# A second feed-forward block's down product turned round, and a final norm taken by token

## Chip, cores and metric

One core of one Trainium2 chip runs the whole program. The metric is device time in microseconds (us), median of the runs shown.

## What is computed

One layer on 512 tokens of width 1024, all in float32: a feed-forward block, a token mixer, a second feed-forward block, and a norm.

```python
x = x + 0.5 * swiglu(rmsnorm(x, ffn1_norm), ffn1_w_gate, ffn1_w_up, ffn1_w_down)
x = x + token_mixer(rmsnorm(x, mix_norm), w_in, w_out, ...)
x = x + 0.5 * swiglu(rmsnorm(x, ffn2_norm), ffn2_w_gate, ffn2_w_up, ffn2_w_down)
return rmsnorm(x, final_norm)
# swiglu(x, g, u, d) = (silu(x @ g) * (x @ u)) @ d, hidden width 2816 = 22 tiles of 128
```

## The kernel before

Between the stages x lies turned: eight tiles `x[k]` of 128 features by 512 tokens. Every product is made of three matmuls (`mm3`, L125): each operand is split into a high part (a cast to fp32r on ScalarE, ACT) and a rest (value minus high part, a subtraction on VectorE, DVE), and high times high, high times rest and rest times high are added in a PSUM bank. TensorE (PE) runs the matmuls, SyncE (SP) and GpSimd (POOL) issue the loads.

A feed-forward block (`ffn`, L207) first computes gate and up products of hidden tiles 0 to 3 with 512 tokens moving (L688 to L717), then hands over to `pipeline` (L636). That one works through a list of **units** (L304 to L322):

- a g or u unit, named by its first hidden tile (g4, g6, u6, g8, ...): the gate or up product of two hidden tiles, done as a two-by-two block product with **seven** products in place of eight. Its steps are in `SEVEN` (L46), named by the weight side: a11, s3, s2, a12, s1, a22, s4. A step is 12 matmuls, 256 tokens moving, and goes to one of four banks w, x, y, z. After a11 the bank w is copied into x, after s2 x into y (L464, L466, ACT), so that later steps add to them: seed copies.
- a d unit: the down product of two output tiles over a group of eight hidden tiles, by the same seven steps. There are two groups (hidden tiles 6 to 13 and 14 to 21) and four d units in each.
- a p unit: an output tile's down product over the first six hidden tiles, in the plain way: 18 matmuls, 512 tokens moving. In the second block, output tiles 6 and 7 do this at the very end by halves of the tokens (l and r, L472), so that the norm of the first half runs beside the second.

The second block's order is g4; g6,u6 to g12,u12; three p; four d; g14,u14 to g20,u20; three p; four d; l and r.

The order on every engine is written out by hand, from a calendar: `starts` gives each step a nominal time (a step is 1410 ns), and events are put at times before it and sorted (`at`, L413). For step t the weight cast on ACT (`high`, L380) is queued four steps ahead, the rest on DVE (`low`, L396) three steps ahead, the sum of weights that s2 and s4 need (`total`, L370) five steps ahead, and a unit's loads seven ahead (L656). Two weight sums of a unit (for s1 and s3) come from memory: SP loads one block, and POOL issues a load that adds the other (L342). Raw weights have three buffers; the split ones have room for six steps. Engines take their queues strictly in this order, each as fast as its inputs come.

`kept` (L542) turns a pair's two activations into what a d unit needs: sums of their four blocks, high parts and rests, 4 operations on ACT and 8 on DVE. Pair (4,5) only gets plain high parts and rests (L558), and so do the single tiles 0 to 3 (`activated`, L223).

After the last group each finished x tile is squared, weighted by the norm's gain and, by halves of the tokens, scaled by the factor; the right half is transposed on TensorE in the end (L1396 to L1549). The output is put together from the two halves.

Of the kernel before, what the change touches and what calls it, by code (L numbers as in the profile page):

```python
# [21 lines left out]
P = 128  # L22
# [31 lines left out]
STEP, PLAIN_STEP, HALF_STEP = 1410, 4080, 2130  # L54
# [12 lines left out]
def tile_macaron(ctx: ExitStack, tc, xs, xT, wf, wgu1, wst1, wd1, wdg1, wqk, wvw, wv, wo, wgu2, wst2, wd2,  # L67
                 wdg2, lams, relb, addc, out):
# [138 lines left out]
    def ffn(wgu, wst, wd, wdg, n0, n1, norm, early, res, nm, hooks, ended, first=None,  # L207
            bias=None, last=None, bank_of_last=None):
# [20 lines left out]
        def gate(j, pg, pu):  # L229
            t1 = tp.tile([P, S], F32, tag="ptb", name=f"t1{nm}{j}")  # L230
# [10 lines left out]
            activated(j, t1)  # L241
# [56 lines left out]
        ups, up_w = {}, {}  # L298
# [5 lines left out]
        units = [("g", n1)]  # L304
        for j in range(n1 + 2, PLAIN + 8, 2):
            units += [("g", j), ("u", j)]
        plain = 5 if last is None else 3
        units += [("p", m) for m in range(plain)] + [("d", 0, m) for m in range(0, KD, 2)]
        for j in range(PLAIN + 8, JF, 2):
            units += [("g", j), ("u", j)]  # L310
        units += [("p", m) for m in range(plain, KD if last is None else KD - 2)]
        units += [("d", 1, m) for m in range(0, KD, 2)]
        if last is not None:
            units += [(h, m) for h in "lr" for m in (KD - 2, KD - 1)]
        ops, begin, starts, now = [], {}, [], 0
        for u in units:
            begin[u] = len(ops)
            for o in ((u[0],),) if u[0] in "plr" else SEVEN:
                ops.append((u, o))
                starts.append(now)  # L320
                now += {"p": PLAIN_STEP, "l": HALF_STEP, "r": HALF_STEP}.get(u[0], STEP)
        starts.append(now)  # L322
# [7 lines left out]
        def sum_slots(u):  # L330
            if u[0] == "d":
                return GROUP_SUMS[u[2] // 2 % 2]
            if u == units[0]:
                return PAIR_SLOTS[0][:2]
# [5 lines left out]
        sums, raws, second, made, half, g, hs = {}, {}, {}, {}, [], {}, {}  # L340
# [12 lines left out]
        def load(u):  # L353
            raws[u] = []
            whole = [wd[u[1]]] if u[0] in "pl" else [rows(u)[0], rows(u)[1][:, 512:]]
            for a in whole:
# [4 lines left out]
        def source(t):  # L361
            u, o = ops[t]
            r0 = raws[u][0]
            if o[0] in ("p", "l"):
                return r0[:, :PLAIN * P]
# [4 lines left out]
        def total(t):  # L370

            u, o = ops[t]
# [6 lines left out]

        def high(t):  # L380
            u, o = ops[t]
            if o[0] in ("p", "l"):
                half.clear()
                h, l = w_place(ODD * (o[0] == "l"))
                made[t] = h[:, :PLAIN * P], l[:, :PLAIN * P]
            else:
                if not half:
                    h, l = w_place(ODD)
                    half.extend([(h[:, :512], l[:, :512]), (h[:, 512:], l[:, 512:])])
                    if t and ops[t - 1][1][0] == "p":  # L390
# [5 lines left out]
        def low(t):  # L396
            h, l = made[t]
            V.tensor_tensor(l, source(t), h.bitcast(F32), op=ALU.subtract)  # L398

# [37 lines left out]
        def product(t):  # L437
            u, o = ops[t]
            if o[0] in ("l", "r"):
                half_product(t, u[1], o[0])  # L440
# [31 lines left out]
        def half_product(t, m, o):  # L472
            c = left if o == "l" else right
            h, l = made[t] if o == "l" else made[t - 2]
            begun = m == KD - 1
            po = bank_of_last(int(o == "r")) if begun else mm_bank(f"p{o}{nm}{m}")
            for k in range(PLAIN):
                w = slice(k * P, (k + 1) * P)
                mm3(po[:, :HS], h[:, w], l[:, w], ah[k][:, c], al[k][:, c],
                    k == 0 and not begun, k == PLAIN - 1, begun)  # L480
                last(starts[t], m, o, k, put)
            if not begun:
                put(starts[t + 1], stt, x[m][:, c], po[:, :HS], 0.5, x[m][:, c], ALU.add)
            last(starts[t + 1], m, o, PLAIN, put)

        def bank_tags(u):


            seq = [v for v in units if v[0] not in "plr"]
# [52 lines left out]
        def kept(j, t1, t0, t2):  # L542
# [11 lines left out]
            def parts(t, h, l, a):  # L554
# [3 lines left out]
            if j < PLAIN:  # L558
                for r, t in ((1, t1), (0, t2)):
                    h = ah[j + r] = slot(j + r, f"ah{nm}{j + r}", F32R)  # L560
                    l = al[j + r] = slot(JF + j + r, f"al{nm}{j + r}", F32R)
                    parts(t + STEP, h[:], l[:], g[j][r][:])
                return
            places = [lambda n=n, i=i: slot(i, f"h{n}{nm}{j}", F32R)
                      for n, i in enumerate(PAIR_SLOTS[(j - PLAIN) // 2 % 4])]
            t = {}

            def b11():
                t["b"] = places[0]()
                A.copy(t["b"][:, left], g0[:, left])  # L570

# [4 lines left out]
            def b2_rest():  # L576
                t["l2"] = places[2]()
                rest(t["l2"][:], g1[:], t["h2"][:])

# [4 lines left out]
            def t0_rest():  # L584
                t["l0"] = places[4]()
                rest(t["l0"][:], g0[:], t["h0"][:])

# [4 lines left out]
            def t1_rest():  # L592
                t["l1"] = places[6]()
                rest(t["l1"][:], g1[:], t["h1"][:])
                b = hs[j] = {"b11": (t["b"][:, left], t["b"][:, right])}
                for n, i, c in (("b21", 2, left), ("b22", 2, right), ("t1", 0, left),
                                ("t3", 0, right), ("t4", 1, left), ("t2", 1, right)):
                    b[n] = t[f"h{i}"][:, c], t[f"l{i}"][:, c]

            put(t0 + STEP, b11)  # L600
            put(t0 + 2 * STEP, lambda: rest(t["b"][:, right], g0[:, left], t["b"][:, left]))
            put(t1 + STEP, b2)
            n = max(t1, t2)
            put(n, less, g0[:, left], g0[:, left], g0[:, right])
            put(n + STEP, b2_rest)
            put(n + STEP, less, g0[:, right], g1[:, right], g0[:, right])
            put(n + 2 * STEP, t0_parts)
            put(n + 2 * STEP, stt, g1[:, right], g1[:, right], -1.0, g0[:, left], ALU.subtract)
            put(n + 2 * STEP, stt, g1[:, left], g1[:, right], -1.0, g1[:, left], ALU.subtract)

            at(n + 3 * STEP, 5, t1_parts)
            late = 2 * STEP * (j > n1)
            at(n + 3 * STEP + late, 1, t0_rest)
            at(n + 4 * STEP + late, 1, t1_rest)

        def down_step(t, u, o, banks):
# [16 lines left out]
            if group == 1 and o in ("a22", "s4") and (last is None or m < KD - 2):  # L633
                ended(m + (o == "a22"), t, put)

        def pipeline():  # L636
            seen = {}
            for t, (u, o) in enumerate(ops):
                if o[0] in ("p", "l"):
# [3 lines left out]
                elif o[0] != "r":  # L643
                    if t == begin[u]:
                        if u != units[0]:
# [5 lines left out]
                            if u == ("g", PLAIN + 10):  # L651
# [4 lines left out]
                        at(starts[t] - 7 * STEP, 1.5, load, u)  # L656
# [4 lines left out]
                at(starts[t], 4, product, t)  # L661
            if bias is not None:
# [8 lines left out]
            run(1 << 40)  # L671

# [717 lines left out]
    half_gain = sp.tile([P, 1], F32, tag="keep", name="half_gain", bufs=1)  # L1390
    fin = {}

    def half(hh):
        return slice(hh * HS, (hh + 1) * HS)

    def weighted(m, hh):  # L1396

        g2 = m // 2
        if (hh, g2) not in fin:
            fin[hh, g2] = cp.tile([P, S], F32, tag=f"xh{hh * 4 + g2}", name=f"y{hh}{g2}")  # L1400
        if m == KD - 1:
            A.activation(fin[hh, g2][:, half(m % 2)], fin["x7", hh][:, :HS], AF.Copy,
                         scale=half_gain[:])
            return
        A.activation(fin[hh, g2][:, half(m % 2)], x[m][:, half(hh)], AF.Copy,
                     scale=sm[:, 3 * KD + m:3 * KD + m + 1])

    def tile_ended(m, t, put):

        squared(m, t, put, EPS * D / P if m == 4 else None)  # L1410
        for hh in range(2):
            put(t + 2 * STEP, weighted, m, hh)

    def last(t, m, o, k, put):


        hh = int(o == "r")
        c = half(hh)
        if k == PLAIN:
            q = fin.setdefault("sq", {})  # L1420
            if m not in q:
                q[m] = slot(8 + m - (KD - 2), f"sql{m}")
            if m == KD - 1:
                put(t, lambda: A.activation(q[m][:, c], fin["x7", hh][:, :HS], AF.Square, scale=0.5))
            else:
                put(t, A.activation, q[m][:, c], x[m][:, c], AF.Square)
            put(t, weighted, m, hh)
            if o == "l":
                put(t, lambda: V.tensor_tensor(sq[:, c], sq[:, c], q[m][:, c], op=ALU.add))
            if (o, m) == ("r", KD - 1):  # L1430
                put(t, final_end)
        elif (o, m, k) == ("l", KD - 2, 0):
            A.activation(root[:], eps[:], AF.Sqrt)
            V.tensor_scalar_mul(half_gain[:], gain(3, KD - 1), 0.5)
# [226 lines left out]
```

## Time and profile before

| | us |
|---|---|
| runs: median (lowest to highest) | 925.98 (925.86 to 926.51) |
| profiled execution: span from first to last instruction | 924.1 |
| median less span: what lies around it | 1.9 |
| pipeline of the second block begins | 633.06 |
| its down product begins (first p tile) | 722.51 |
| last weight product ends | 915.71 |

A span is from the first to the last instruction of the program; the time of a run also holds what lies around it. The page names instructions by engine, line and tiles (out<-in). Duration is from start to end of one instruction; where an engine overlaps instructions, the distance between starts is shorter. DMA rows give the microseconds from issue to landing.

### The profile page before, as it was taken

To read this page: it belongs to the slowest core of one execution; us is meant where nothing else is said; L and a number is where in the kernel's file an instruction comes from. 1 tells how busy PE (TensorE), PEld (TensorE's weight loads), DVE (VectorE), ACT (ScalarE), POOL (GpSimd) and SP (SyncE) were. 2 spreads that over 40 slices of the span, in tenths; PEclk is the share of its full clock that TensorE was granted. 3 is DMA by queue.
4 is the path that set the end of the run, shared out by engine and by line. 5 is a ranking of instruction groups with operands and counts; after the bars stand their busy time and mean duration, and the time that the engine had idled before them with its cause. 6 is when DMAs were issued, how large, how long until landed. Compare 5 with 4: busy or idle time off the path is not lost.

```text
span 924.1 us, 16880 instructions
## 1 busy us (share of the span) xinstructions
PE 917.2 (99%) x6286; PEld 847.1 (92%) x6286; DVE 726.3 (79%) x1499; ACT 544.3 (59%) x1134; POOL 98.0 (11%) x116
## 2 busy tenths in 40 slices
PE   9999999999999999999999999999999999999997
PEld 7888999999999998888989778889999999999997
DVE  7797887686888897858866556797888777888784
ACT  7455665355665775656757664455666455666573
POOL 0001101112201100000000003110120012210100
PEclk9999999999999999999999999999999999999999
DMA  7455646578757563524343213464774677875542
GB/s 263 124 146 151 160 124 177 137 184 211 196 133 200 152 173 99 153 75 128 99 137 93 69 63 120 115 180 101 183 191 117 161 203 189 201 196 145 144 129 92
DMA packets 59827, 136.61 MB, mean 148 GB/s; under 512 B 6816, under 2 KB 8096, under 8 KB 59744
## 3 DMA queue, kind: packets, MB, share of 16 engines
q1 hardware_dynamic: 45776, 110.14, 36.7%
q0 software_dynamic: 13968, 25.39, 17.5%
q8 instruction: 49, 0.80, 0.4%
q14 instruction: 34, 0.28, 0.1%
HBM read 130.21 MB, written 2.14 MB: 143 GB/s over the span
## 4 chain that ended last, share of the span: by engine, by line
PE 97%; DVE 1%; DMA 0%; issue 0%; DVEq 0%; ACT 0%; SPq 0%
PE pq L126 2%; PE pwo L126 2%; PE pq L128 2%; PE pq L127 2%; PE pk L126 2%; PE pk L128 2%; PE pwo L127 2%; PE pwo L128 2%; PE pk L127 2%; PE pua L128 2%; PE pua L127 2%; PE pua L126 2%; PE pda L127 1%; PE pda L126 1%; PE pub L126 1%; PE pub L127 1%
## 5 line engine op out<-in xcount | busy, mean ns | idle before, releaser
L1108 ACT ACTIVATE pr<-pr,mx 128x128 f32<-128x128 f32 (+3 forms) x64 | 36.0, 563 | 37.1 <-DVE mx L1105 36.9
L1105 DVE CUSTOM_DVE_ANT_0 pr<-sc,strip 128x128 f32<-128x128 f32 (+3 forms) x64 | 30.6, 487 | 18.9 <-PE sc L1103 18.6
L394 ACT CAST w<-s2b 128x512 fp32r<-128x512 f32 x50 | 31.0, 621 | 16.0 <-DVE s2b L376 14.4
L398 DVE TENSOR_TENSOR w<-s2b,w 128x512 fp32r<-128x512 f32 x50 | 34.2, 684 | 7.3 <-ACT w L394 7.3
L394 ACT CAST w<-s2a 128x512 fp32r<-128x512 f32 x46 | 28.6, 621 | 16.1 <-DVE s2a L376 13.2
L398 DVE TENSOR_TENSOR w<-s2a,w 128x512 fp32r<-128x512 f32 x46 | 31.5, 684 | 6.6 <-ACT w L394 6.6
L153 POOL TENSOR_TENSOR sq<-sq,sqt 128x512 f32<-128x512 f32 x7 | 11.0, 1564 | 237.9 <-ACT sqt L152 237.8
L126 PE MATMUL pq<-xh,w 128*128 128x512 f32 x64 | 26.7, 417 | 0.0
L126 PE MATMUL pwo<-mh,w 128*128 128x512 f32 x64 | 25.6, 400 | 0.0
L912 DVE TENSOR_TENSOR w<-raw_qk,w 128x512 fp32r<-128x512 f32 x28 | 19.0, 687 | 8.2 <-ACT w L908 8.1
L128 PE MATMUL pq<-xh,w 128*128 128x512 f32 x64 | 25.1, 392 | 0.0
L126 PE MATMUL pk<-xh,w 128*128 128x512 f32 x64 | 25.1, 392 | 0.0
L127 PE MATMUL pq<-xl,w 128*128 128x512 f32 x64 | 25.1, 392 | 0.0
L128 PE MATMUL pk<-xh,w 128*128 128x512 f32 x64 | 25.0, 391 | 0.0
L127 PE MATMUL pwo<-ml,w 128*128 128x512 f32 x64 | 25.0, 390 | 0.0
L128 PE MATMUL pwo<-mh,w 128*128 128x512 f32 x64 | 25.0, 390 | 0.0
L127 PE MATMUL pk<-xl,w 128*128 128x512 f32 x64 | 24.9, 390 | 0.0
L1102 PE MATMUL sc<-k,q 128*128 128x128 f32 (+3 forms) x64 | 20.7, 324 | 0.0
L1103 PE MATMUL sc<-l,q 128*128 128x128 f32 (+3 forms) x64 | 20.5, 322 | 0.0
L127 PE MATMUL pwgb<-xl,w 128*128 128x256 f32 x72 | 20.2, 281 | 0.0
L128 PE MATMUL pwgb<-xh,w 128*128 128x256 f32 x72 | 20.2, 281 | 0.0
L127 PE MATMUL pxgb<-ttb,w 128*128 128x256 f32 x72 | 20.2, 281 | 0.0
(728 smaller groups left out, 4010.0 us busy)
## 6 DMA issues: line engine op xcount, KB each, us to landing
raw_qk<-wqk_dram SPq DMA_DIRECT2D x16, 512.0 KB, 3.2
raw0bg<-wst_dram SPq DMA_DIRECT2D x9, 512.0 KB, 4.7
raw_gua<-wgu_dram SPq DMA_DIRECT2D x8, 512.0 KB, 3.3
raw0ag<-wst_dram SPq DMA_DIRECT2D x8, 512.0 KB, 4.8
raw0ad<-wdg_dram SPq DMA_DIRECT2D x8, 512.0 KB, 4.2
strip<-bias_rows SPq DMA_DIRECT2D x16, 256.0 KB, 3.7
raw_wo<-wo_dram SPq DMA_DIRECT2D x8, 512.0 KB, 3.3
raw_gub<-wgu_dram SPq DMA_DIRECT2D x8, 512.0 KB, 3.5
```

The lines of the kernel that those rows point to most:

```text
L126: T.matmul(po, wh, mh, start=first, stop=False, skip_group_check=on)
L127: T.matmul(po, wh, ml, start=False, stop=False, skip_group_check=on)
L128: T.matmul(po, wl, mh, start=False, stop=last, skip_group_check=on)
L153: G.tensor_tensor(sq[:], sq[:], t[:], op=ALU.add)
L394: A.copy(made[t][0], source(t))
L398: V.tensor_tensor(l, source(t), h.bitcast(F32), op=ALU.subtract)
L912: V.tensor_tensor(l[:, c:c + 512], raw[:, c:c + 512], h[:, c:c + 512].bitcast(F32), op=ALU.subtract)
L1102: T.matmul(ps[:, :w], qs[:, qi], ks[:, :w], start=True, stop=False)
L1103: T.matmul(ps[:, :w], qs[:, qi], ls[:, :w], start=False, stop=True)
L1105: V.tensor_tensor_reduce(out=pi, in0=ps[:, :w], in1=st["b"][m][:, w - 1::-1], op0=ALU.add, op1=ALU.min, scale=1.0, scalar=3.0e38, accum_ou ...
L1108: A.activation(pi, pi, AF.Exp, scale=-1.0, bias=st["mx"][:, m, i:i + 1], accum_out=st["ls"][:, m, i:i + 1])
```

## The change

The second block's down product is turned: for tokens by output features, an activation block (128 hidden by 128 tokens) is the stationary side and the weights move, 512 output features wide. All 22 hidden tiles now go by seven products, as 11 pairs: a two-by-two block product of (two token halves by two hidden tiles) with (two hidden tiles by two feature halves). There are two turned blocks: t0 over pairs 0, 2, 4, 6, 8, and t1 over pairs 10 to 20, a pair being named by its first tile. The order is g4; g6,u6; g8,u8; t0; g10,u10 to g20,u20; t1. In a block, each of the seven products runs over all its pairs before the next one starts; a step of one pair is `mm3` for two token tiles, 6 matmuls of 512. The p, l and r units are gone, and so are the d units of this block (the first block keeps its own).

x is transposed by TensorE in u8: 32 transposes of 128x128, in two lots, copied back by ACT into the same eight tiles, which then hold tokens by features: tile 4*dh+tt is token tile tt, feature half dh. The banks of a turned block are added to them by DVE.

All pairs' activations go through `kept`; those of tiles 0 to 3 stay in slots from the gate on and are split in g4 to g8, 0.75 steps apart. Loads of raw weights of a pair unit are put seven and five steps ahead, in place of both at seven.

The final norm has tokens on partitions: a square with a sum along the row on ACT, a factor of one column on DVE and ACT, and one operation on DVE that scales by the factor and by a broadcast copy of the gain. In t1's last product (s4) tile 2's matmuls run before tile 3's, so that tile 2 is finished beside them; tiles 0 and 1 are finished after a22. The output is written as it is.

```diff
+        else:
+            units = [("g", n1)] + pairs(n1 + 2, TURNED_PAIRS[0][-1] + 2) + [("t", 0)]
+            units += pairs(TURNED_PAIRS[1][0], JF) + [("t", 1)]
...
             for o in ((u[0],),) if u[0] == "p" else SEVEN:
+                for p in range(len(TURNED_PAIRS[u[1]])) if u[0] == "t" else (0,):
+                    ops.append((u, o, p))
+                    starts.append(starts[-1] + (PLAIN_STEP if u[0] == "p" else STEP))
...
+        def block_product(t):
+            u, o, p = ops[t]
+            ps = TURNED_PAIRS[u[1]]
...
+            pw, pz, pv = b[:2], b[2:4], b[4:]
+            banks = {"a11": pw, "s2": pw, "a22": pw, "s3": pz, "s1": pz, "s4": pz, "a12": pv}[o[0]]
...
+            block_mms(banks, o, ps[p], p, n, h, l, (0, 1))
+            if p == n - 1:
+                block_step(starts[t + 1], u, o[0], pw, pz, pv)
+
+        def block_mms(banks, o, j, p, n, h, l, tiles):
+            fresh = o[0] in ("a11", "s3", "a12")
+            bh, bl = hs[j][o[2]]
+            for tt in tiles:
+                c = slice(tt * P, (tt + 1) * P)
+                mm3(banks[tt], bh[:, c], bl[:, c], h, l, fresh and p == 0, p == n - 1, not fresh)
+
+        def block_step(t, u, o, pw, pz, pv):
+            def into(tt, dh, bank, f):
+                y = x[4 * dh + tt]
+                put(t, stt, y, bank, f, y, ALU.add)
+            for i in range(2):
+                if o == "a11":
+                    into(i, 0, pw[i], 0.5)
+                elif o == "s3":
+                    into(i, 1, pz[i], -0.5)
+                    into(2 + i, 1, pz[i], -0.5)
+                elif o == "s2":
+                    put(t, A.copy, pz[i], pw[i])
...
+        def turn(dh):
+            turned = [mm_bank(f"xt{dh}{tt}") for tt in range(NQ)]
+            for tt in range(NQ):
+                for k in range(4):
+                    T.transpose(turned[tt][:, k * P:(k + 1) * P], x[4 * dh + k][:, tt * P:(tt + 1) * P],
+                                ident[:])
...
+            if final is not None:
+                for dh in range(2):
+                    time = starts[begin["t", 0] - 6 + 3 * dh]
+                    at(time, 5, turn_x, time, dh)
+                for n, j in enumerate((0, 2)):
+                    kept(j, 0, (2 + 9 * n) * STEP, 0, 0.75)
...
+        def block_events(t):
+            u, o, p = ops[t]
+            now = starts[t]
...
+            at(now - 4 * STEP, 3, high, t)
+            at(now - 3 * STEP, 2.5, low, t)
...
+    def factor(tt):
+        v, r, w, h, y = (number(n, tt) for n in (3, 4, 5, 6, 7))
+        V.scalar_tensor_tensor(v, number(1, tt), 1.0 / D, number(2, tt), op0=ALU.mult, op1=ALU.add)
+        A.activation(r, v, AF.Sqrt)
+        V.scalar_tensor_tensor(w, r, r, v, op0=ALU.mult, op1=ALU.add)
+        V.reciprocal(w, w)
+        V.tensor_tensor(h, r, w, op=ALU.mult)
+        V.tensor_tensor(y, h, h, op=ALU.add)
...
+        elif what == "a22":
+            for tt in (0, 1):
+                put(t, square, 1, tt, x[4 + tt])
+            for tt in (0, 1):
+                put(t, factor, tt)
+            for tt in (0, 1):
+                put(t, left_out, tt)
+        elif what.startswith("s4") and what.endswith("1"):
+            i = int(what[3])
+            square(1, 2 + i, banks[i], 0.5)
+            factor(2 + i)
+            right_out(2 + i, banks[i])
```

In the new code the cast is L435, the rest L439, the weight sum L398 (turned) and L403, L405, the add into x L530, the seed copies L518, the transposes L629.

More of the change, by code (lines that the diff above doesn't have):

```diff
@@ L296, in up_weights, with pairs @@
             up_w[j] = get_w(wst[j - n1][1], f"su{nm}{j}")
-        ups, up_w = {}, {}
+        ups, up_w, g = {}, {}, {}
         left, right = slice(0, HS), slice(HS, S)
[L304 to L315, printed above, removed]
+        def pairs(j0, j1):
+            return [(h, j) for j in range(j0, j1, 2) for h in "gu"]
+        plain = 5
+        if final is None:
+            units = [("g", n1)] + pairs(n1 + 2, PLAIN + 8)
+            units += [("p", m) for m in range(plain)] + [("d", 0, m) for m in range(0, KD, 2)]
+            units += pairs(PLAIN + 8, JF)
+            units += [("p", m) for m in range(plain, KD)] + [("d", 1, m) for m in range(0, KD, 2)]
+        else:
+            units = [("g", n1)] + pairs(n1 + 2, TURNED_PAIRS[0][-1] + 2) + [("t", 0)]
+            units += pairs(TURNED_PAIRS[1][0], JF) + [("t", 1)]
+        ops, begin, starts = [], {}, [0]
         for u in units:
             begin[u] = len(ops)
[L318 to L322, printed above, removed]
+            for o in ((u[0],),) if u[0] == "p" else SEVEN:
+                for p in range(len(TURNED_PAIRS[u[1]])) if u[0] == "t" else (0,):
+                    ops.append((u, o, p))
+                    starts.append(starts[-1] + (PLAIN_STEP if u[0] == "p" else STEP))
         def rows(u):
@@ L338, in sum_slots @@
             return PAIR_SLOTS[(u[1] - PLAIN) // 2 % 4][o:o + 2]
-        sums, raws, second, made, half, g, hs = {}, {}, {}, {}, [], {}, {}
+        sums, raws, second, made, half, hs = {}, {}, {}, {}, [], {}
         def weight_sums(u):
@@ L351, in weight_sums, with load @@
                 sums[u].append(t)
[L353 to L356, printed above, removed]
+        def load(u, which=(0, 1)):
+            raws.setdefault(u, [])
+            whole = [wd[u[1]]] if u[0] == "p" else [rows(u)[0], rows(u)[1][:, 512:]]
+            for a in [whole[i] for i in which if i < len(whole)]:
                 t = wp.tile([P, 1024], F32, tag="raw", name=f"raw{len(raws[u])}{nm}{u[0]}")
@@ L400, in moving, with kept_weights @@
+        keeps = {}
+        def kept_weights(p):
+            if p < 4:
+                w = tp.tile([P, 5 * HS], F32R, tag=f"pr{p % 2}", name=f"kw{nm}{p}")
+            else:
+                if "tx" not in keeps:
+                    keeps["tx"] = tp.tile([P, 12 * HS], F32R, tag="tx", name=f"kx{nm}", bufs=1)
+                w = keeps["tx"][:, (p - 4) * 1024:(p - 3) * 1024]
+            return w[:, :512], w[:, 512:1024]
         def moving(u, block):
@@ new lines, in turn, with turn_x @@
+        def turn(dh):
[4 more added lines that the diff above has]
+                                ident[:])
+            return turned
+        def turn_x(t, dh):
+            turned = turn(dh)
+            for tt in range(NQ):
+                put(t + STEP * (tt // 2), A.copy, x[4 * dh + tt], turned[tt][:])
@@ L486, in bank_tags @@
         def bank_tags(u):
-            seq = [v for v in units if v[0] not in "plr"]
+            seq = [v for v in units if v[0] != "p"]
             n = seq.index(u)
@@ L594, in t1_rest, with b11_rest @@
                 rest(t["l1"][:], g1[:], t["h1"][:])
[L595 to L598, printed above, removed]
+                block(("t4", "1"), left)
+                block(("t2", "1"), right)
+                hs[j] = b
+            def b11_rest():
+                rest(t["b"][:, right], g0[:, left], t["b"][:, left])
@@ L671, in pipeline @@
             run(1 << 40)
+        def block_events(t):
+            u, o, p = ops[t]
+            now = starts[t]
+            if o[0] in ("s3", "s1"):
+                at(starts[begin[u]] - TURNED_AHEAD[o[0]][u[1]][p] * STEP, 1, block_load, u, o[0], p)
+            elif o[0] == "a11":
+                at(now - 7 * STEP, 2.2, block_load, u, o[0], p)
+            elif o[0] in ("a12", "a22"):
+                at(now - 8 * STEP, 1.5, block_load, u, o[0], p)
+            if (u[1], o[0]) == (1, "s4"):
+                now = starts[begin[u]] + (20 + 3 * p) * STEP
+            if o[0] in ("s2", "s4"):
+                at(now - 5 * STEP, 2, total, t)
+            at(now - 4 * STEP, 3, high, t)
+            at(now - 3 * STEP, 2.5, low, t)
+            if t == begin[u] and u[1] == 1:
+                at(now + 2 * STEP, 1, final, "begin", now + 2 * STEP, put, None)
         j0 = 0
@@ L1448, in bank_begun @@
-    def bank_begun(hh):
-        fin["x7", hh] = mm_bank(f"px7{hh}")
-        A.activation(fin["x7", hh][:, :HS], x[KD - 1][:, half(hh)], AF.Copy, scale=2.0)
-    def final_sums(hh, src, first, end):
-        n = NQ // 2
-        if first:
-            fin["ps", hh] = pp.tile([P, S], F32, tag="mm", name=f"st_n4{hh}", bufs=4)
-        for i in range(n):
-            c = slice((hh * n + i) * P, (hh * n + i + 1) * P)
-            T.matmul(fin["ps", hh][:, i:i + 1], src[:, c], ones_d[:, 0:1], start=first and i == 0, stop=end,
-                     skip_group_check=True)
```

398 lines of the change are left out of this document (219 added, 179 removed).

## Prediction

> **What bounds the kernel now.** I read the page first, for the engine that never rests and for the chain of work that ended last.
>
> ```profile
> span 924.1 us, 16880 instructions
> PE 917.2 (99%) x6286; PEld 847.1 (92%) x6286; DVE 726.3 (79%) x1499; ACT 544.3 (59%) x1134; POOL 98.0 (11%) x116
> ...
> PEclk9999999999999999999999999999999999999999
> ...
> PE 97%; DVE 1%; DMA 0%; issue 0%; DVEq 0%; ACT 0%; SPq 0%
> ```
>
> TensorE (PE) is busy for 99% of the span at full granted clock, and the chain runs through it. A saved TensorE microsecond is a saved microsecond, if VectorE (DVE) keeps up. Next comes busy time by stretch: stretch, its length, then busy time (count) of PE, PEld, DVE, ACT, POOL, then clock, DMA share and GB/s.
>
> ```profile
> 601.09:620.13 19.04, 19.04 (x86) 15.77 (x84) 18.98 (x31) 9.65 (x15) 2.03 (x3) 1.00 0.59 171
> 643.00:662.87 19.87, 19.87 (x170) 19.87 (x169) 15.40 (x28) 13.06 (x29) 3.43 (x4) 1.00 0.73 179
> 662.87:682.75 19.88, 19.88 (x170) 19.88 (x169) 17.54 (x34) 12.76 (x28) 3.48 (x4) 1.00 0.64 169
> 722.51:734.81 12.30, 12.30 (x57) 10.14 (x55) 9.57 (x17) 4.99 (x9) 1.74 (x2) 1.00 0.56 147
> 734.81:774.57 39.76, 39.76 (x338) 39.76 (x336) 31.62 (x60) 20.44 (x41) 6.94 (x8) 1.00 0.69 175
> 854.09:866.38 12.29, 12.29 (x56) 10.14 (x55) 9.56 (x17) 4.98 (x9) 1.75 (x2) 1.00 0.56 145
> 866.38:906.14 39.76, 39.76 (x337) 39.76 (x336) 33.52 (x63) 27.93 (x57) 3.48 (x4) 1.00 0.45 120
> 906.14:915.55 9.41, 9.41 (x82) 9.41 (x81) 3.98 (x14) 3.81 (x12) 0.00 (x0) 1.00 0.01 2
> ```
>
> By the kernel's order these are: gate and up products 512 wide; g6,u6; g8,u8; three p tiles; four d units; three p tiles; four d units; the l and r halves. TensorE has no gap in any. But VectorE has only 4.5 us of idle time in the second row and 2.3 us in the third: in the pairs it is nearly the bound itself. Its queue in g8, and the product that uses its work (start, duration):
>
> ```profile
> 666.60 0.68 DVE L398 TENSOR_TENSOR w<-s1bg,w 128x512 fp32r<-128x512 f32 x1
> 667.20 0.42 DVE L435 SCALAR_TENSOR_TENSOR g1b<-g1b,g0b 128x256 f32<-128x256 f32 x1
> 667.65 0.42 DVE L435 SCALAR_TENSOR_TENSOR g1b<-g1b 128x256 f32<-128x256 f32 x1
> 667.99 0.68 DVE L398 TENSOR_TENSOR w<-raw1bg,w 128x512 fp32r<-128x512 f32 x1
> 668.60 0.68 DVE L398 TENSOR_TENSOR w<-s2b,w 128x512 fp32r<-128x512 f32 x1
> 669.20 0.68 DVE L376 TENSOR_TENSOR s2b<-s1bu,raw0bu 128x512 f32<-128x512 f32 x1
> ...
> 668.55 0.28 PE L126 MATMUL pygb<-txb,w 128*128 128x256 f32 x1
> ```
>
> Two things are to be seen. First, a 512-wide operation takes 0.68 us but the next starts 0.60 us after it; a 256-wide one costs 0.34, or 0.45 where the next reads its result. Second, the rest (L398) of g8's s1 weights ends at 667.28 and its product starts at 668.55: the lead is 1.27 us, and in these rows TensorE never waits for it.
>
> **Part by part.** (1) Down product. Out go 6 p tiles, 8 d units and the halves: 12.30+39.76+12.29+39.76+9.41 = 113.5 us. In come 11 pairs x 7 products x 2 token tiles x 3 = 462 matmuls 512 wide. Their price is that of 601.09:620.13: 28 groups of three, each on another bank, in 19.04 us, 0.2267 each; so 104.7 us. (The p tiles, 54 in 12.30, give 0.2278.) The gain is **8.8 us**: fewer columns (236,544 for 245,760), and 256 columns cost 0.118 (1.42 us for 12), more than half of 0.227. Token tiles as stationary change nothing in the count: each matmul loads its stationary side in before too (PEld count).
>
> (2) The 32 transposes of x stand in u8, in TensorE's order, with nothing beside them.
>
> ```profile
> 916.81 1.94 PE L1509 MATMUL ft<-ident,y 128*128 128x128 f32 x16
> ...
> L1509 PE MATMUL ft<-ident,y 128*128 128x128 f32 x16 | 1.9, 275 | 0.0
> ```
>
> Sixteen took 1.94 us with the last one's own end: 0.11 each, **+3.5 us**. The eight copies back are ScalarE's; ACT is busy for 64% of g8,u8.
>
> (3) VectorE in g6 to g8. The added work is that pairs (0,1) and (2,3) are now also split into the four-block sums of the seven products (a pair: 3 operations 512 wide, 5 of 256), and pair (4,5) goes the same way instead of two plain rests. I count VectorE's queue from the rest of g6's first weights up to that of g8's s1: 28 wide and 13 half-wide operations in before, 35 and 27 now. At 0.603 and 0.337, with six dependent steps of 0.11, that is 30.9 us, against 18 steps x 1.42 = 25.6. It starts with the 3 steps (4.26) that it is queued ahead, less 0.68 for the last one itself: 3.6. So the rest is 5.3-3.6 = 1.7 us late, and TensorE waits for it. Lower bound: 1.3, if some of the idle time ahead of g6 is used. Upper bound: 3.0, if the stretch must also keep the 1.27 us of lead that before still has at its end. I take **+1.9**, near the sum, since a late engine finds the banks that it reads already full. The wait ends in u8, which has little of such work and the transposes.
>
> (4) VectorE in the turned blocks. After the last a11 product x is added from two banks, after s3 from four (L530 of the new code, the same operation as this row, 512 wide):
>
> ```profile
> L435 DVE SCALAR_TENSOR_TENSOR x<-pdb,x 128x512 f32<-128x512 f32 x6 | 4.1, 692 | 5.7 <-PE pdb L128 5.7
> L394 ACT CAST w<-s2b 128x512 fp32r<-128x512 f32 x50 | 31.0, 621 | 16.0 <-DVE s2b L376 14.4 <-PE pdb L127 1.5
> L835 ACT ACTIVATE sqd<-x 128x512 f32<-128x512 f32 x5 | 3.1, 624 | 2.0 <-DVE x L435 2.0
> L502 ACT ACTIVATE g1b<-rbc_n 128x512 f32<-128x512 f32 x9 | 5.7, 632 | 5.1 <-DVE rbc_n L426 4.6
> L423 ACT COPY pxgb<-pwgb 128x256 f32<-128x256 f32 x9 | 3.2, 357 | 7.1 <-PE pwgb L128 7.1
> ```
>
> Queued behind these adds are the rests of the coming weights. In the first block, from the end of a11 to the rest for the fourth s2 product stand 19 wide operations, a half-wide and a dependent one: 12.3 us and 0.3 for hops, against 8 products x 1.361 = 10.9. So TensorE waits **1.7** there (1.2 to 2.2). In the second block 20 wide ones and 0.8 make 13.2 against 9 x 1.361 = 12.3: **+1.0** (0.6 to 1.4). Elsewhere the sum of a block leaves VectorE free: 35 steps of 1.361 hold 62 wide operations and 8 half-wide, 40 of 47.6 us.
>
> (5) Loads. Seven loads of 256 KB a pair replace the down weights of before, at 192 GB/s in a block (9.2 MB in 47.7 us), where pairs ran at 179.
>
> ```profile
> raw0bg<-wst_dram SPq DMA_DIRECT2D x9, 512.0 KB, 4.7
> s3bg<-wst_dram POOLq DMA_DIRECT2D x9, 256.0 KB, 5.8
> ```
>
> I followed SP's queue past each buffer's last reader: the tightest is the first weights of g10, in whose place the first block's raw weights lie until four steps (5.6 us) before the cast needs them; 4.7 fits. SP and POOL otherwise run well ahead. I cost it at nothing; if a load lands 2 us later, the lead of g10 takes it, and the upper bound is those 2 us. Gates 0 to 3, freed from their casts ahead of g4, gain nothing: TensorE is dense there.
>
> (6) The end.
>
> ```profile
> 915.43 0.28 PE L128 MATMUL px<-ahb,w 128*128 128x256 f32 x1
> ...
> 916.99 0.17 ACT L1469 ACTIVATE lt<-st_n 128x2 f32<-128x2 f32 x1 [0.48 <-PE st_n L1462]
> 917.19 0.34 DVE L1473 SCALAR_TENSOR_TENSOR lw<-lt,st_n 128x1 f32<-128x1 f32 x2
> 917.57 0.17 DVE L1475 RECIPROCAL lw<-lw 128x2 f32<-128x2 f32 x1
> 917.77 0.16 DVE L1476 SCALAR_TENSOR_TENSOR ly<-lt,lw 128x2 f32<-128x2 f32 x1
> 918.02 1.46 ACT L1518 ACTIVATE o<-ft,ly 128x512 f32<-128x512 f32 x2 [0.86 <-DVE ly L1476]
> 918.55 2.32 SPq L1523 DMA_DIRECT2D out_dram<-o  x5
> ```
>
> From the last weight product's end (915.71) to the end of the span are 8.4 us. The new end: tile 2's factor waits on VectorE behind the outputs of tiles 0 and 1 (four 512-wide operations, then five small ones of 0.2), and ScalarE's copy for tile 2 behind that factor, so its square of tile 3 starts about 0.7 late (counted from the end of a22, 8.2 us earlier); square 0.65; factor 1.2; first half out 0.5; three issues 0.48 apart (five begin in 2.32-0.4 us), and what follows the last one's begin as in before (924.1-920.4 = 3.7). That is 0.7+0.65+1.2+0.5+1.0+3.7 = 7.75, **-0.65** (from -1.5 to +0.5).
>
> Sum: -8.8+3.5+1.9+1.7+1.0-0.65 = **-1.35 us**, so a span of 922.75. The span is 924.1 where the median of the runs is 925.98, with 1.9 us around it: **924.6 us**.
>
> **Rivals.** (a) VectorE's lateness does not reach TensorE. For it: before reaches leads of over 3 us, and the first half of each turned block is light. Against: the third row, where VectorE is full. The three waits of 4.6 then shrink to 0 to 1.5: 920.0 to 921.5.
>
> (b) The end on the other side: ScalarE's seed copies, in u6, g8 and u8. Product s2 needs px copied from pw, and in ScalarE's order that copy stands behind a Silu or cast that waits for VectorE: after VectorE's result come 0.63, a half-wide operation, a cast 0.62 and the copy 0.36, pipelined some 1.7 us, while the rest of the weights takes 0.6. Where VectorE is already as late as its lead, each such unit adds 1.1, and g6 too; four make +4.4: 929.0. For it: ACT waited 5.1 us for rbc_n in before. Against: a wait at s2 gives VectorE the same time back, and it needs it two steps later anyway. It decides from a VectorE lead below 1.1 us.
>
> (c) A page's rule. VectorE's next operation starts only when the one before is through: 0.68 and 0.42 each. Counted so, the queue up to g8's s1 is 35.3+0.7 us against 25.6, and its wait 6.8 instead of 1.7; in the blocks 19 x 0.08 and 20 x 0.08 come on top, some 3 in all: 933. The Trainium skill, "VectorE: DVE Perf Modes", The DRAIN you can't avoid, says this; the six rows above speak against it, except for the dependent one.
>
> (d) The change does not do what it says: 512 wide costs twice the 256-wide price (0.2367). Then 109.4 replace 113.5: 929.3. The p tiles speak against it.
>
> (e) A transpose costs its duration, 0.275, not the distance to the next: 8.8 us for 3.5, 929.9. The Trainium skill, "TensorE: Matmul & The Clock Gate", Part 4: PE-mode transpose, gives about 275 ns for one in a kernel. The row of durations agrees, and that of sixteen in 1.94 us says that they overlap.
>
> **How the numbers follow.** A measurement of this kernel can tell about 0.2% (1.85 us) from no change. The sum as it stands, between 924.13 and 927.8 with its bounds: 0.42. Faster by more: 0.35, of it rival (a) 0.22, and 0.13 for my sum with the bounds on the low side (waits of 3.1, the end at -1.5: 922.3). Slower by more: 0.23, of it (b) 0.16, (c) 0.03, (d) 0.02, (e) 0.02. The sum's own range, bounds all on one side, is 922.3 to 927.8. To hold 8 in 10 it reaches from 920.3 (rival a at its best lies below) to 929.2 (half of b, and c to e, above).
>
> **What would show it.** TensorE's idle time between 640 and 672 near 1.9 us, ended by DVE L439; another 1.7 and 1.0 in the fourth s2 product of the blocks; blocks of 0.227 per matmul; transposes 0.11 apart; 7.7 us behind the last product. No idle time there would show (a); idle time of s2 products ended by ACT L518, (b). Wrong altogether would be idle time ended by a DMA.

## The result and the profile after

| | median | runs, lowest to highest | profiled execution |
|---|---|---|---|
| before | 926.34 us | 7, 925.75 to 926.57 | span 924.1 |
| changed | 929.57 us | 7, 928.34 to 931.55 | span 927.8 |

The changed kernel is slower by 0.4%: ratio 1.0036, 95% interval 1.0025 to 1.0047. Forecast were 924.6 us, a little faster, with a range from 920.3 to 929.2. The page of the changed kernel, with the parts that were shown of before:

```profile
span 927.8 us, 16132 instructions
PE 914.2 (99%) x5892; PEld 826.7 (89%) x5892; DVE 736.8 (79%) x1518; ACT 545.4 (59%) x1130; POOL 104.5 (11%) x124
...
PE 88%; DVE 8%; DMA 2%; issue 1%; SPq 1%; ACT 1%; POOL 0%; DVEq 0%; POOLq 0%; ACTq 0%
```

TensorE has 3.0 us less to do, and the span is 3.7 us longer. The chain, 97% TensorE before, now runs for 12% through other units: through VectorE, and for 2% through transfers. Where that is, the table by stretch shows (stretch, length, busy time of PE, PEld, DVE, ACT, POOL, then the granted clock): g6; u6; g8; u8; the first turned block; the pairs g10 to u20; the second turned block; and four microseconds out of that block.

```profile
644.04:656.78 12.74, 10.58 (x87) 10.13 (x86) 12.52 (x26) 9.59 (x21) 1.75 (x2) 1.00 0.45 130
656.78:667.06 10.28, 10.20 (x87) 9.99 (x86) 10.21 (x20) 7.26 (x15) 1.82 (x3) 1.00 1.00 236
667.06:676.99 9.93, 9.93 (x86) 9.93 (x85) 9.86 (x21) 6.53 (x14) 3.43 (x4) 1.00 0.98 220
676.99:690.72 13.73, 13.69 (x119) 13.49 (x118) 7.23 (x14) 9.74 (x22) 3.47 (x4) 1.00 0.93 244
690.72:739.32 48.60, 47.91 (x213) 39.34 (x212) 40.88 (x69) 24.03 (x42) 4.33 (x5) 1.00 0.52 129
739.32:858.59 119.27, 119.27 (x1009) 119.27 (x1008) 101.50 (x189) 74.19 (x156) 24.47 (x28) 1.00 0.83 203
858.59:921.28 62.69, 60.22 (x254) 47.96 (x252) 51.83 (x102) 33.31 (x66) 4.59 (x6) 0.97 0.40 118
884.00:888.00 4.00, 4.00 (x12) 3.12 (x11) 4.00 (x8) 1.67 (x4) 0.00 (x0) 0.57 0.00 0
```

The first block is 1.0 us above its 35 x 1.361 = 47.6, the pairs are as before, and the second block is 5.5 above its 42 x 1.361 = 57.2 (0.2 of it is the end of the last matmul). In g6 VectorE is busy for 12.52 of 12.74 us and TensorE for 10.58. The last row is new: for four microseconds the granted clock is 0.57.

I call a wait the distance between the starts of two matmuls, less the 0.227 or 0.118 that it is without one. In g6 there are two waits of 1.3, with the 0.1 by which the next matmul starts late:

```profile
651.10 0.39 PE L139 MATMUL pygb<-txb,w 128*128 128x256 f32 x1 [1.12 <-ACT pygb L518]
655.25 0.39 PE L139 MATMUL pygb<-xh,w 128*128 128x256 f32 x1 [1.04 <-DVE rbc_n L521]
```

With 0.1 in s2 this makes 2.8 us, and at the end of u6 0.35 come on top. The releasers are to be noted: not a rest (L439), but a seed copy on ScalarE, and the addition on VectorE that reads the bank of s1 before s4 may add to it.

In the second block, VectorE's queue (start, duration), and TensorE from the first two matmuls of the fourth s2 product on, of which the second reads the rest:

```profile
872.51 0.69 DVE L398 TENSOR_TENSOR rab<-sCb,rab 128x512 f32<-128x512 f32 x1
...
878.53 0.68 DVE L439 TENSOR_TENSOR w<-rab,w 128x512 fp32r<-128x512 f32 x1
879.14 2.47 DVE L530 SCALAR_TENSOR_TENSOR x<-pt,x 128x512 f32<-128x512 f32 x4
881.53 0.68 DVE L398 TENSOR_TENSOR rab<-sCb,rab 128x512 f32<-128x512 f32 x1
882.13 1.89 DVE L439 TENSOR_TENSOR w<-rab,w 128x512 fp32r<-128x512 f32 x3
```

```profile
880.63 0.40 PE L139 MATMUL pt<-w,h5b 128*128 128x512 f32 x1
882.87 0.50 PE L140 MATMUL pt<-w,h5b 128*128 128x512 f32 x1 [1.83 <-DVE w L439]
...
884.13 0.55 PE L139 MATMUL pt<-w,h5b 128*128 128x512 f32 x1
884.48 0.63 PE L140 MATMUL pt<-w,h5b 128*128 128x512 f32 x1
884.91 0.63 PE L141 MATMUL pt<-w,h6b 128*128 128x512 f32 x1
```

The four adds after s3 stand in one piece ahead of the rest for the fourth s2 product, as the prediction had it, and that product's second matmul waits 2.1 us. Then, 1.3 us after TensorE is at work again, nine matmuls take 3.64 us from start to start in place of 2.04, seven of them 0.43 each in place of 0.227: half clock, which costs 1.6 us.

Two smaller waits (0.4 and 0.6) stand in a11, at the very start of the block. ScalarE's casts there (start, duration, and in brackets its idle time and what ended it), the queues of POOL and SP, and the issues grouped, with the median time to landing:

```profile
854.46 0.62 ACT L435 CAST w<-rab 128x512 fp32r<-128x512 f32 x1 [0.45 <-PE pwub L140]
860.50 1.21 ACT L435 CAST w<-rab 128x512 fp32r<-128x512 f32 x2 [5.42 <-DMA rab<-wdg_dram]
...
863.60 0.62 ACT L435 CAST w<-rab 128x512 fp32r<-128x512 f32 x1 [0.54 <-DMA rab<-wdg_dram]
```

```profile
849.66 2.75 POOL L482 DMA_DIRECT2D sCb<-wdg_dram  x3 [7.15 <-DVE w L439]
```

```profile
851.23 0.33 SPq L481 DMA_DIRECT2D sCb<-wdg_dram  x1
851.61 1.42 SPq L470 DMA_DIRECT2D rab<-wdg_dram  x2
```

```profile
rab<-wdg_dram SPq DMA_DIRECT2D x6, 256.0 KB, 8.0
```

The a11 weights (rab) are late by transfer. Ahead of them go the weight sums of s1 (sCb), which are first read at 872.51, by the sums for s2 in VectorE's queue above: POOL issues three of the adding loads at once, SP puts another ahead, and a load of 256 KB takes 8.0 us.

The end, on ScalarE and VectorE, with the last weight product:

```profile
920.89 0.39 PE L141 MATMUL pt<-kxb,h2b 128*128 128x512 f32 x1
```

```profile
921.37 0.60 ACT L1615 ACTIVATE junk<-pt 128x512 f32<-128x512 f32 x1
...
922.09 0.16 DVE L1623 SCALAR_TENSOR_TENSOR fin<-fin 128x1 f32<-128x1 f32 x1 [0.77 <-ACT junk L1615]
...
923.25 0.87 DVE L1640 SCALAR_TENSOR_TENSOR x<-pt,fin,gb 128x256 f32<-128x256 f32 x2
```

From the end of the last product (921.28) to the end of the span are 6.5 us, where before had 8.4: the square begins 0.1 after the product, not 0.7, and 3.2 us follow the begin of the last issue, not 3.7.

One more difference lies far from the change. The pipeline of the second block begins at 634.10 here, 1.04 later than before, and all of that arises in the first 7 us of the program, where the starts of the first products lie 0.37 to 0.59 apart in place of 0.23. The instructions there are the same in both kernels.

### The profile page after: what moved, and what is told of

Read it like the earlier page. It is cut to its first block, busy times and chain, and to the rows that moved or that the text cites. A ratio compares the mean times of both kernels' runs of the same rounds, so it can differ in the third digit from the quotient of the medians.

```text
span 927.8 us, 16132 instructions
## 1 busy us (share of the span) xinstructions
PE 914.2 (99%) x5892; PEld 826.7 (89%) x5892; DVE 736.8 (79%) x1518; ACT 545.4 (59%) x1130; POOL 104.5 (11%) x124
## 4 chain that ended last, share of the span: by engine, by line
PE 88%; DVE 8%; DMA 2%; issue 1%; SPq 1%; ACT 1%; POOL 0%; DVEq 0%; POOLq 0%; ACTq 0%
DVE w L439 3%; PE pt L140 2%; PE pt L141 2%; PE pt L139 2%; PE pq L139 2%; PE pwo L139 2%; PE pq L141 2%; PE pq L140 2%; PE pk L139 2%; PE pk L141 2%; PE pwo L140 2%; PE pk L140 2%; PE pwo L141 2%; PE pua L139 2%; PE pua L140 2%; PE pua L141 2%
## 5 line engine op out<-in xcount | busy, mean ns | idle before, releaser
L435 ACT CAST w<-s2a 128x512 fp32r<-128x512 f32 x46 | 28.6, 621 | 15.0 <-DVE s2a L403 12.1
L439 DVE TENSOR_TENSOR w<-s2a,w 128x512 fp32r<-128x512 f32 x46 | 31.5, 685 | 6.6 <-ACT w L435 6.6
L435 ACT CAST w<-rab 128x512 fp32r<-128x512 f32 x27 | 16.7, 629 | 25.1 <-DVE rab L398 16.7
L439 DVE TENSOR_TENSOR w<-s2b,w 128x512 fp32r<-128x512 f32 x34 | 23.3, 686 | 9.8 <-ACT w L435 9.8
L435 ACT CAST w<-s2b 128x512 fp32r<-128x512 f32 x34 | 21.1, 621 | 7.6 <-DVE s2b L403 5.2
L530 DVE SCALAR_TENSOR_TENSOR x<-pt,x 128x512 f32<-128x512 f32 x26 | 17.1, 686 | 9.3 <-PE pt L141 9.3
L371 POOL DMA_DIRECT2D s1bg<-wst_dram x9 | 7.8, 868 | 126.3 <-DVE w L439 54.2
L140 PE MATMUL pt<-w,h5b 128*128 128x512 f32 x44 | 18.1, 411 | 2.5 <-DVE w L439 2.5
```

Source lines behind the costliest of these rows:

```text
L140: T.matmul(po, wh, ml, start=False, stop=False, skip_group_check=on)
L371: nc.gpsimd.dma_start(t[:], b, accum_op=ALU.add)
L435: A.copy(made[t][0], source(t))
L530: V.scalar_tensor_tensor(o, a, f, b, op0=ALU.mult, op1=op1)
```

## The experiments

The theories after this profile: the wait in the second block is made by late loads, by the adds, or by both; that in g6 by VectorE's total backlog, by what is crowded into g6, or by ScalarE's order; the half clock by TensorE's idle time or by something else. All times below are medians; the ratio is to before.

**e1, the loads.**

```diff
-                "s1": ((12, 9, 6, 4, 1), (12, 9, 7, 5, 2, -1))}
+                "s1": ((12, 9, 6, 4, 1), (4, 3, 2, 1, 0, -1))}
```

> Only the loads of the second turned block's s1 weight sums are put later (from 12 to -1 steps ahead of the block to 4 to -1), so that they no longer stand ahead of its six a11 loads. Theory (late loads): the changed kernel's two waits in a11 (1.06 us) go, VectorE loses no time there (it idled 2.6 and 1.5 us), so the wait in s2 shrinks from 2.1 to about 1.0 us, the 0.4 in s3 goes, and the half clock behind it (1.6 us) does not come: about 4 us less than 929.6, 925.5. Rival (VectorE's queue alone): only the 1.06 in a11 goes, 928.5. Second rival (the transfers are limited by the DMA engines whatever their order): the a11 loads still land later than 860, 929.6.

Measured: 924.92 us (10 runs), ratio 0.999 (0.998 to 1.0001). In its profile the a11 loads take 5.1 us, the waits in a11 and s3 are gone, and the wait of the fourth s2 product is 1.6 us with no half clock behind it.

```profile
rab<-wdg_dram SPq DMA_DIRECT2D x6, 256.0 KB, 5.1
```

So the order of the loads was at fault, not the transfers' sum. Of the waits in the changed kernel's profile, late loads made 1.06 in a11, 0.4 in s3 and 0.5 in s2; 1.6 belongs to the adds alone, more than the 1.0 expected. The a11 part varies from run to run: with the loads in their old order, the profiles of e2, e3, e5, e6 and e8 below lose 0 to 0.5 us there (their a11 loads take 6.8 to 7.7 us) and 0.4 to 0.6 in s3; with the later loads, e7 and e9 lose nothing in either.

**e2, the adds.**

```diff
-            def into(tt, dh, bank, f):
+            def into(tt, dh, bank, f, late=0):
...
-                put(t, stt, y, bank, f, y, ALU.add)
+                put(t + late * STEP, stt, y, bank, f, y, ALU.add)
...
-                    into(i, 1, pz[i], -0.5)
-                    into(2 + i, 1, pz[i], -0.5)
+                    into(i, 1, pz[i], -0.5, 2 * i + 0.5)
+                    into(2 + i, 1, pz[i], -0.5, 2 * i + 1.5)
```

> Only the four adds into x after s3 are spread, one a step behind that step's rest, in both turned blocks. Theory (the adds ahead of the rests make the wait): three adds of 0.60 us less stand ahead of the rest of the fourth s2 product; the first block's wait of 0.96 goes, the second's of 2.1 falls to about 0.3, no half clock (1.6), the 1.06 in a11 stays: 4.3 us less, 925.3. Rival (the late loads alone make the second block's wait): 0.96 less in the first block, and a wait of over 1.5 us and the half clock stay in the second: 928.6.

Measured: 925.09 us (10 runs), ratio 0.9986 (0.9976 to 0.9995). VectorE in the second block:

```profile
877.25 0.68 DVE L439 TENSOR_TENSOR w<-rab,w 128x512 fp32r<-128x512 f32 x1
877.85 0.68 DVE L530 SCALAR_TENSOR_TENSOR x<-pt,x 128x512 f32<-128x512 f32 x1
878.45 0.68 DVE L439 TENSOR_TENSOR w<-rab,w 128x512 fp32r<-128x512 f32 x1
879.05 0.68 DVE L530 SCALAR_TENSOR_TENSOR x<-pt,x 128x512 f32<-128x512 f32 x1
```

Adds and rests alternate, the same work in another order, and both blocks' s2 waits are gone, the second's in spite of late loads (0.4 each stay in a11 and s3). The rival, loads alone, is out.

**e3, the splitting earlier.**

```diff
-                    kept(j, 0, (2 + 9 * n) * STEP, 0, 0.75)
+                    kept(j, 0, (-3 + 8 * n) * STEP, 0, 0.75)
```

> Only the splitting of pairs (0,1) and (2,3) is put earlier: from step -3 and 5 on in place of 2 and 11, into the 4.6 us in which VectorE idles at the start of g4. Theory (VectorE's backlog): the 3.15 us of waits in g6 to u6 and at g8 fall below 0.4: 926.7. Rival (ScalarE's order: the seed copy behind a cast that waits for VectorE): only the wait that VectorE's add ends (1.2) goes, the 1.28 ended by a seed copy stays: 928.3.

Measured: 928.42 us (10 runs), ratio 1.0026 (1.0017 to 1.0036). My theory fell: work was taken into VectorE's idle time ahead of g6, and the waits are 3.1 us as they were, all of them now in g6, at the same two places.

```profile
652.05 0.39 PE L139 MATMUL pygb<-txb,w 128*128 128x256 f32 x1 [0.99 <-ACT pygb L518]
656.67 0.39 PE L139 MATMUL pygb<-xh,w 128*128 128x256 f32 x1 [1.51 <-DVE rbc_n L521]
```

What the move did besides: with pair (0,1) out of g6, it put all of pair (2,3) between g4's end and g6's, beside the splitting of (4,5).

**e6, the splitting around g6.**

```diff
-                    kept(j, 0, (2 + 9 * n) * STEP, 0, 0.75)
+                    kept(j, 0, (-3 + 16 * n) * STEP, 0, 0.75)
```

> Only the splitting of pairs (0,1) and (2,3) is moved, as in e3, but pair (2,3) now behind g6, into u6: from step -3 and 13 on in place of 2 and 11. Theory (VectorE's crowd in g6 alone: in the stretch of its seven steps stand rests, weight sums, pair (4,5)'s splitting and parts of both other pairs, 13.8 us against 9.9): about 3 us of operations leave g6, the 3.1 us of waits there and in u6 fall below 0.5: 926.9. Rival (the lateness only moves on into u6 and g8, where pair (6,7) is split): half of it stays, 928.3. Second rival (ScalarE's seed copy): 1.3 stays in g6 whatever VectorE's queue: 927.9.

Measured: 928.56 us (10 runs), ratio 1.0008 (0.9992 to 1.0024). The waits fall from 2.8 to 0.5 in g6, and 0.9 stays in u6 and 0.3 in g8: 1.7 in all for 3.1. So the crowd in g6 made most of g6's waits, but 0.8 of the 2.3 us that leave g6 come back in u6 and g8: the first rival is right, about half of the whole stays. The seed copy ends no wait any more, so ScalarE's order needs VectorE's lateness to matter. The time alone would not have told, since the median is hardly below the changed kernel's: the runs lie in two groups (four from 924.6 to 926.2, six from 928.5 to 929.6), and the profiled one, of 928.85, has 2.3 us lost in the first 10 us of the program and the half clock again, behind a wait of 2.05:

```profile
882.90:886.90 4.00, 4.00 (x12) 3.09 (x12) 4.00 (x8) 2.03 (x4) 0.00 (x0) 0.57 0.00 0
```

**e5, the wait filled.**

```diff
+            if (u, o[0], p) == (("t", 1), "s2", 3):
+                fill = mm_bank("fill")
+                for i in range(8):
+                    T.matmul(fill[:], hs[ps[2]][o[2]][0][:, :P], made["last"], start=True, stop=True)
             h, l = made.pop(t)
+            made["last"] = h
```

> Eight matmuls 512 wide, whose result nobody reads, are put ahead of the fourth s2 product of the second turned block, where TensorE waits 2.1 us; nothing else changes. Theory (the idle time brings the half clock): the product begins when it did, the granted clock stays 1.00 behind it, 1.6 us less: 928.0. Rival (the half clock has another cause): it stays, 929.6, or the fillers add to the time: up to 931.

Measured: 928.35 us (10 runs), ratio 1.0019 (1.001 to 1.0028). The table by stretch shows the fillers, and the 8 us behind the wait at full clock:

```profile
879.91:881.73 1.82, 1.82 (x10) 1.50 (x8) 1.82 (x4) 0.12 (x1) 0.00 (x0) 1.00 1.00 384
882.00:890.00 8.00, 7.95 (x35) 6.49 (x35) 8.00 (x15) 6.81 (x13) 0.00 (x0) 1.00 0.01 5
```

This agrees with idle time as the cause, and is no proof: the wait of 2.1 stands unfilled in four profiled executions, and the half clock follows it in two (changed, e6) and not in two (e3, e8). A wait of 1.6 (e1) wasn't followed by it.

The traces tell the two kinds apart. In the changed kernel the granted clock falls at 884.21, is back 3.41 us later, and falls again behind the last matmul, at 925.17: 12 x 3.413 us after the first fall. In e6 the two falls (883.35 and 924.31) lie as far apart. So I cut the traces into windows of 3.413 us, counted back from that last fall (923.79 in e3, 921.01 in e8). These hold the wait: one window in the changed kernel, one in e6, two in e3, two in e8:

```profile
880.79:884.21 3.42, 1.59 (x8) 1.13 (x7) 3.42 (x7) 1.89 (x4) 0.00 (x0) 1.00 0.50 186
879.94:883.35 3.41, 1.52 (x7) 1.02 (x6) 3.41 (x7) 1.74 (x4) 0.00 (x0) 1.00 0.44 168
879.41:882.82 3.41, 2.44 (x11) 1.68 (x9) 3.41 (x7) 0.62 (x1) 0.00 (x0) 1.00 0.89 302
882.82:886.24 3.42, 2.48 (x11) 2.06 (x12) 3.42 (x7) 2.88 (x6) 0.00 (x0) 1.00 0.26 99
876.63:880.05 3.42, 3.07 (x14) 2.15 (x12) 3.42 (x7) 0.62 (x1) 0.00 (x0) 1.00 0.96 310
880.05:883.46 3.41, 1.87 (x8) 1.55 (x9) 3.41 (x7) 2.27 (x5) 0.00 (x0) 1.00 0.24 93
```

Where the wait lies whole in one window, TensorE is idle for 1.83 and 1.89 us of it, and the next window runs at half clock. In e3 and e8 a boundary cuts the wait, no window holds more than 1.54 us of idle time, and the clock stays. In none of the other windows of the eleven traces, from the first full clock to the last product, is TensorE idle for longer than that, and none is followed by half clock. So whether an execution loses the 1.6 us depends on where the wait falls in the windows; this is read from the traces, and no run moved the windows. The filled execution itself says little: in e5 (last fall 921.92) a boundary at 880.96 would have cut the wait in any case.

The Trainium skill, "TensorE: Matmul & The Clock Gate", Part 1: The HAM clock gate, says that the clock falls to half after at least one idle window of about 3.4 us, that the window runs freely, and that it is released after a busy one. The traces agree on the window's length (3.41 us) and on its running freely, since its boundaries lie elsewhere in each execution; on the idle time they differ, a window of which 1.8 us were idle was enough.

**b1, e8 and e9, the beginning.** e8 is the changed kernel and e9 the next one below, both with one line:

```diff
-WARM = 8
+WARM = 10
```

> The kernel before, unchanged, for one more look at its first microseconds: in the profiles of the changed kernel and its variants the second block's pipeline begins 0.2 to 2.1 us later than in the one of before (633.06), by matmuls at half clock at the very start. If that is chance from run to run, it shows here too, by 0 to 2 us; if it belongs to the changed program, the pipeline begins within 0.2 us of 633.06.

> The changed kernel with 10 warming matmuls at the very start in place of 8; nothing else. In the profiles of the changed kernel and its variants 0 to 11 of the first products run at half clock, behind 0.5 to 0.9 us in which TensorE stands idle after the warming, and the second block's pipeline begins at 633.3 to 635.4; in the two of before none does, and it begins at 633.07. Theory (the idle time brings it): no product runs at half clock, the pipeline begins at 633.5 or earlier, and the time is 0.5 to 1 us less than 929.6. Rival (another cause): the beginning still lies between 633.3 and 635.4, the time within 0.3 of 929.6.

> The same two warming matmuls more in the kernel with all three moves (921.17). Theory: its profile began at 633.43, so there is little to gain in the median, 0.2 us, 921.0. Rival: the two matmuls stand ahead of the first product and cost up to their own 0.4 us: 921.6.

Measured: b1 925.9 us, pipeline from 633.08; e8 928.78 (5 runs, 926.74 to 930.12), from 633.83; e9 921.33 (4 runs), from 633.84. Both profiled executions of before have a quick start, all nine of the changed kernel and its variants one that is 0.2 to 2.3 us slower. But 3 of 14 runs of before that were made beside e6 took 928.2 to 928.8, so before isn't free of losses of this size. Without any idle time ahead of the first product two matmuls still ran at half clock in e8, so idle time isn't the whole cause there. So e8's theory isn't borne out, and its 0.8 us less lie within the spread of the runs; in e9 the two matmuls gain nothing either. The windows have a part in it: TensorE begins its warming at 1.0 us in all eleven traces, and full clock comes at a boundary of the windows, at 4.3 and 4.0 us in the two of before and at 5.0 to 9.5 in the nine others. Each time it is the end of the first window of which TensorE was idle for less than 0.5 us (the windows ahead of it hold 0.53 or more). In e8 that is 6.2, since a boundary at 2.8 cuts its warming in two. Why before nearly always starts quickly stays open; it is worth about 1 us in the profiled execution.

**e7, all three moves** (e1, e2 and e6).

> The later loads of e1, the spread adds of e2 and the splitting of e6 together; nothing is left out. If the causes add up: from 929.6 go 1.06 (a11), 0.4 (s3), 2.1 (s2), 1.6 (half clock) and 0.96 (first block), and 2.7 in g6: 920.8, below both kernels. Rival (the causes overlap, since all three are VectorE's lateness, which only surfaces at another place): 922.5 to 924.

Measured: 921.17 us (5 runs, 920.77 to 921.79), ratio 0.9942 (0.9929 to 0.9955), below both kernels. Of its page:

```profile
span 919.4 us, 16137 instructions
PE 910.5 (99%) x5892; PEld 825.6 (90%) x5892; DVE 736.3 (80%) x1518; ACT 545.5 (59%) x1130; POOL 104.3 (11%) x124
```

TensorE's waits in the two blocks are gone, and in g6 to g8 the 1.7 us of e6 stay. VectorE does as much as in the changed kernel (736.3 us for 736.8). The 8.4 us between the two medians come from the order of the work (at most some 0.7 from the beginning, which was that much quicker in this profile), and the causes add up: the rival's 922.5 to 924 is out. Of the 8.8 us expected, g6 to g8 gave 1.4 in place of 2.7. The second block takes its 57.3 us:

```profile
855.53:912.86 57.33, 57.33 (x254) 47.11 (x252) 51.56 (x102) 31.91 (x63) 6.15 (x8) 1.00 0.45 135
```

## Why the prediction was wrong, step by step

| step | forecast | changed kernel | what the runs show |
|---|---|---|---|
| (1) down product | -8.8 | -8.8 | 0.227 a matmul, both blocks |
| (2) transposes | +3.5 | +3.3 | 16 in 1.67; 0.5 more in u8 by waits |
| (3) g6 to g8 | +1.9 | +3.1 | VectorE's crowd in g6; e6 leaves 1.7 |
| (4) adds | +2.7 | 1.0 and 2.5 | 1.0 and 1.6 with loads in time (e1) |
| (5) loads | 0 | 1.06, and 0.9 of the 2.5 above | e1 removes both; other runs 0 to 0.5 for the 1.06 |
| half clock | none | +1.6 | behind a wait of 2.1 within one window |
| (6) end | -0.65 | -1.9 | square 0.1 late, not 0.7; 3.2 behind the last issue, not 3.7 |
| beginning | none | +1.0 | other runs 0.2 to 2.3 |

(1) held to 0.1 us, and with it rival (d) is out. (2) held: the transposes start 0.109 apart, and rival (e) is out:

```profile
L629 PE MATMUL xt<-ident,x x32: 270/272/273, 679.8 to 687.8; 128*128 128x128 f32 x32
```

(3) failed in its mechanism: I counted VectorE's queue over 18 steps, from g6 to g8's s1, and put the wait at a rest there. The queue is uneven, and TensorE waits where it is longest, in g6. There it meets the bank's reader and the seed copy, not a rest. Rival (b) was half right: one wait of 1.3 is ended by the copy, but one unit has it, not four. (The 5.1 us that (b) counts as ScalarE's wait for rbc_n are its whole idle time there; 4.6 were for rbc_n.) Rival (a), that the lateness doesn't reach TensorE, is out; rival (c) too, since the 512-wide operations still start 0.60 apart.

(4) was right in place and kind, and in sum: 2.6 with loads in time, for 2.7. The parts were mis-sized, 1.0 for 1.7 in the first block and 1.6 for 1.0 in the second.

(5) is the step that failed most. "I cost it at nothing" rested on following each buffer's last reader; it didn't ask what else the queues issue at that time. The loads of the second block's a11, not those of g10, are the tight ones. They cost 1.06 by themselves and 0.9 through VectorE, which idles for them and then comes late to its adds: the 2 us that I gave as upper bound. The range left them out: with these 2 us, the bounds all on one side reach 929.8, not 927.8. They also made the 1.6 of the adds into the 2.1 behind which the half clock came. That I hadn't asked for at all: a wait of TensorE was priced at its length, and here it cost 1.6 more. Of the 5.05 us between the span forecast (922.75) and the one measured, the loads are 1.9, the half clock 1.6, (3) 1.2, the beginning 1.0, u8's waits less the transposes' gain 0.3; (6) gave 1.25 back, (4) 0.1, and 0.3 isn't placed.

## What to carry to other kernels

When work on an engine is in order and nearly full, count its queue in the densest stretch, not on average, and look for readers that are in no hurry (here the adds into x) standing ahead of those that TensorE waits for: spreading them took 4.5 us off by itself, the half clock behind the wait included. When a transfer is moved, ask what is issued beside it in the same ten microseconds, not only whether its buffer is free. Price a long wait of TensorE with what may follow it, the half clock, and not only by its length.

## What was not expected of the hardware

A wait of TensorE of 2.1 us was followed, 1.3 us after its end, by 3.4 us at half clock in two of four profiled executions, which made it 3.7 us; one of 1.6 wasn't. What told the two kinds apart was whether the wait fell whole into one of the windows of 3.413 us at whose boundaries the clock changes: 1.83 us of idle time in one window were enough, 1.54 were not. And loads of 256 KB took 6.8 to 8.0 us to landing where the loads for s1, three of them adding ones, were issued just ahead of them, and 5.1 where those came later (e1).
